# Transfers that add into on-chip memory in place of some VectorE sums of weight blocks, and a new order of some products

## The chip, the cores and the metric

The kernel runs on one core of one Trainium2 chip. The metric is the device time of one execution in microseconds (us). It is compared with the time of the kernel before, which is 1497.2 us (median of three runs, 1497.01 to 1497.43).

## The reference

The reference is one layer of a hybrid decoder: a token mixer with two parallel branches, and a squared-ReLU MLP. 256 tokens and 16 learned meta tokens pass through it, with 2048 channels, all in float32.

```python
def hybrid_mixer(xn, w_in, ...):
    proj = xn @ w_in                                  # 2048 x 13336
    ...                                               # forgetting attention, gated linear attention
    y = jax.nn.sigmoid(gate_fox) * (o_fox @ w_o_fox) + jax.nn.sigmoid(gate_gla) * (o_gla @ w_o_gla)
    return y @ w_out
def squared_relu_mlp(xn, w1, w2):                     # 2048 -> 8192 -> 2048
    return jnp.square(jax.nn.relu(xn @ w1)) @ w2
...
    h = h + hybrid_mixer(rmsnorm(h, norm_mix_g[l]), ...)
    h = h + squared_relu_mlp(rmsnorm(h, norm_mlp_g[l]), w_ff1[l], w_ff2[l])
```

Nearly all of the work is matrix products of 256 tokens with large weight matrices. Every weight is read once from HBM.

## The kernel before

**Precision.** Each float32 operand is split into a high part, which ScalarE (ACT) rounds to TensorE's reduced float32, and a low part, which VectorE (DVE) forms as value minus high part. A product is then three matmuls: high by high, high by low, low by high. For weights this split is `cut` (lines 968 to 974): the cast on ACT is line 972 and the subtraction on DVE line 973. It reads a raw tile of 128 x 1024 floats (512 KB) and writes a tile `w`. There are five `raw` buffers and five `w` buffers.

**Stages.** The input projection, both branches and their heads come first, up to about 480 us. From 480 to 698 us `columns` makes, for three groups `b` of output columns, the branch projections (`lone`, tiles `gla` and `fox`) and the two gates (a pair, below). Then the last columns of the mixer and the output projection run to about 840 us, and from there to 1440 us the MLP runs as fifteen pairs. The last output columns and the final norm end the kernel.

**A pair** (`pair_of`) multiplies the operand with two groups of four blocks of 128 columns, `f1` and `f2 = f1 + 4`. The tokens are two halves of 128. The contraction over 2048 runs in steps of 256. A plain step (`plain`) loads one raw tile, splits it, and makes two products of six matmuls of 512 columns, one for each half of the tokens. For the first 512 (one form) or the first 1024 (two forms) of the contraction, a Strassen-Winograd form makes seven products of six matmuls where plain steps make eight. With r11, r21 the weights of `f1` and r12, r22 those of `f2` in the two halves of these 512, a form multiplies

- own tokens with r11 (`m1`), r21 (`m2`), and r21 less the weight sum of `m6` (`m4`);
- sums of tokens, made ahead by `token_sums`, with r12 - r11 (`m5`), r22 - (r12 - r11) (`m6`), r22 - r12 (`m7`) and r22 (`m3`).

The weight sums are made by `less` (line 977): one DVE operation over a whole 128 x 1024 tile. `held` loads r12 and r22 into tiles that stay (`hb`, `hc`; with a second form also `hd`, and `he`, which is the tile `sums4` in the MLP and shows as `sums` in the profile). The fifteen pairs of the MLP are twelve with one form and three with two (`nq == 2`); the three pairs of `columns` have two forms as well. That makes twelve pairs with one form and six with two.

**What sets the order.** SyncE (SP) issues the weight loads in program order; each waits until its `raw` buffer is free, which is when the DVE has read it. ACT and DVE run in order. While the plain steps of one pair run, the steps of the next pair are put between them by lists of places: the `n`-th number is the plain step after which step `n` of the next pair is emitted. Lines 1149 and 1152 hold the lists of `columns`, line 1367 those of the MLP, by `index % 4` of the running pair; `index % 4 == 2` is where the steps of a pair with two forms are emitted. A planner with its own times may move instructions of an engine against each other where nothing forbids it; `keep_in_program_order` holds the results of `less` in place.

**GpSimd (POOL)** has little to do here. Once for each group of the MLP it reloads saved token sums from HBM (line 1378: four transfers of 256 KB, `s_x<-kept_sums`), each waiting until TensorE has used the old ones.

Of the kernel before, what the change touches and what calls it, by code (L numbers as in the profile page):

```python
# [12 lines left out]
ALU = mybir.AluOpType  # L13
# [3 lines left out]
P = 128  # L17
# [56 lines left out]
def trunk(ctx: ExitStack, tc: tile.TileContext, hT, w_small, w_all, consts, w_alpha2, out):  # L74
    nc = tc.nc
# [236 lines left out]
    x = x_row[:, :, NM : NM + 2 * NT].rearrange("p k (o t) -> p k o t", t=NT)  # L312
# [85 lines left out]
    for s in range(KT // 2):  # L398
# [5 lines left out]
        for kk in range(2):  # L404
            k = 2 * s + kk
# [496 lines left out]
    def token_sums(dst, src, temp):  # L902

        v = temp.rearrange("p (s k m) -> p s k m", s=4, m=P)
        c, d = (v[:, i].rearrange("p k (c r) -> p k c r", r=32) for i in (0, 1))
        s3, s4 = (v[:, i].rearrange("p k (c r) -> p k c r", r=32) for i in (2, 3))
        nc.vector.tensor_tensor(c, src(0, 1), src(1, 1), op=ALU.add)
        nc.vector.tensor_tensor(s3, src(0, 0), src(0, 1), op=ALU.subtract)
        nc.vector.tensor_tensor(d, c, src(0, 0), op=ALU.subtract)
        nc.vector.tensor_tensor(s4, src(1, 0), d, op=ALU.subtract)  # L910
        split_to(dst[:, :, :, 0, :], dst[:, :, :, 1, :], v)

# [60 lines left out]
        made(copied, nc.vector.tensor_tensor(lo, r, hi.bitcast(F32), op=ALU.subtract).ins, 1)  # L973
        return [t.rearrange("p k c m -> p k (c m)") for t in (hi, lo)]

    def less(dst, a, b):
        tc.keep_in_program_order(nc.vector.tensor_tensor(dst, a, b, op=ALU.subtract))

    hold_pool = [None]
    held_at = {}  # L980
# [1 line left out]
    def holder(tag):  # L982
        if tag in held_at:
            return held_at[tag]
        return hold_pool[0].tile([P, HK * P], F32, tag=tag, name=nm(tag))
# [13 lines left out]
    def pair_of(f1, x, sums, evict, even, by_rows=False, low=False):  # L999
# [12 lines left out]
        def product(n, xs, w, start=False):  # L1012
            product_into(bk(n), xs, w, start)

        def own(t, k0):
            return tokens(x, t, k0)

        def split_of(raw):
            return cut(raw, low)
# [9 lines left out]
        nq = len(sums)  # L1029

        def held(q):
            got["b", q], got["c", q] = fetched(f2, 4 * q, ("hb", "hd")[q]), fetched(f2, 4 * q + 2, ("hc", "he")[q])

        def m1(q):
            r11 = fetched(f1, 4 * q)
            w = split_of(r11)
            got["a", q] = r11 if nq > 1 else holder("hd")
            less(got["a", q], got["b", q], r11)
            product("x", own(0, 4 * q), w, q == 0)
            if q == nq - 1:  # L1040
                nc.scalar.copy(bk("y"), bk("x"))

        def m5(q):
            w = split_of(got["a", q])
            if nq > 1:
                less(got["b", q], got["c", q], got["b", q])
                less(got["c", q], got["c", q], got["a", q])
            else:
                less(got["a", q], got["c", q], got["a", q])
            product("v", summed(q, 0), w, q == 0)  # L1050
            if q == nq - 1:
                got["m5"] = hold_pool[0].tile([P, 512], F32, tag="m5", name=nm("m5"))
                nc.scalar.copy(got["m5"], bk("v"))

        def m6(q):
            w = split_of(got["c" if nq > 1 else "a", q])
            if nq == 1:
                less(got["b", q], got["c", q], got["b", q])
            product("x", summed(q, 1), w)
            if q == nq - 1:  # L1060
                nc.vector.tensor_tensor(bk("z"), bk("x"), got["m5"], op=ALU.add)
# [9 lines left out]
        def m2(q):  # L1071
            r21 = fetched(f1, 4 * q + 2)
            w = split_of(r21)
            t2 = got["c" if nq > 1 else "a", q]
            less(t2, r21, t2)
            product("y", own(0, 4 * q + 2), w)

        def m4(q):
            product("x", own(1, 4 * q + 2), split_of(got["c" if nq > 1 else "a", q]))

        if nq == 1:
            firsts = [(m, 0) for m in (held, m1, m5, m6, m7, m3, m2, m4)]
# [22 lines left out]
    def columns():  # L1105
# [40 lines left out]
            work += made_pairs[b][1]  # L1146
            work += [lambda b=b, k=k: lone(b, "fox", k) for k in range(0, KT // 2, 2)]
        at = {}
        for n, i in enumerate((-1, 1, 1, 2, 3, 4, 5, 5, 6, 7, 8, 8, 9, 9, 10, 12)):
            at.setdefault(i, []).append(made_pairs[0][0][n])  # L1150
        for b in (1, 2):
            for n, i in enumerate((-5, -4, -3, -1, 0, 2, 3, 4, 5, 6, 7, 8, 9, 10, 10, 12)):
# [211 lines left out]
    while rest_now:  # L1364
        key, make = next(coming, (None, None))
        steps_next, rest_next = make() if make else ([], [])
        at = {1: (0, 3, 4, 5, 6, 8, 9, 10), 2: (0, 2, 1, 2, 4, 5, 5, 6, 7, 7, 8, 8, 9, 9, 10, 11),
              3: (0, 2, 4, 5, 5, 6, 6, 7)}.get(index % 4, (0, 2, 3, 4, 5, 7, 9, 10))
        if index == 0:
            steps_now[7]()  # L1370
        closing = index == 4 * NG - 3
        for i, run in enumerate(rest_now):
            run()
            if index == 0 and i == 2:
                norm2()
            if index % 4 == 3 and i == 0:
                for q in range(4):
                    nc.gpsimd.dma_start(s_x2[:, q].bitcast(F32), kept_sums[:, q])
            for n, step in enumerate(steps_next):
                if at[n] == i and closing and n > 4:  # L1380
                    late.append(step)
                elif at[n] == i:
                    step()
            if not steps_next and i in (1, 3, 5):
                late.pop(0)()
        issued()
        rest_now, index = rest_next, index + 1
# [169 lines left out]
```

## Time and profile before

| | |
|---|---|
| median of three runs | 1497.2 us |
| the profiled execution, its own time | 1497.08 us |
| its span, first to last instruction | 1495.1 us |
| TensorE (PE) busy | 1484.9 us |
| PE weight loads (PEld) busy | 1322.2 us |
| VectorE (DVE) busy | 1193.2 us |
| ScalarE (ACT) busy | 878.4 us |
| GpSimd (POOL) busy | 119.8 us |
| moved by DMA | 335.00 MB |

Matmuls overlap in the array, so a single one shows some 380 ns while the next starts 220 ns after it. A row of the timeline gives start, duration, engine, line, operation, output and inputs, how many such instructions follow each other, and in brackets the idle time before them with what ended it. "Landing" is the time from the issue of a transfer to its completion.

### The profile page before, as it was taken

The numbers are of one execution on the slowest core, as the hardware profiler recorded it, in microseconds if no ns is written. First come the engines' busy times: TensorE is split into PE (matmuls) and PEld (weight loads), VectorE is DVE, ScalarE is ACT, GpSimd is POOL, SyncE is SP. The second block draws the span as 40 slices with busy tenths as digits, with TensorE's granted clock in tenths as the row PEclk, the third lists the DMA queues.
The fourth block names the chain that finished last, engine by engine and source line by source line (L and its number), as shares of the span: only waits on it lengthen the run. The fifth ranks groups of instructions, "written<-read, shape, count | busy, mean of one in ns | idle before, by whom it ended". The sixth has DMA issues, their size and how long they took to land.

```text
span 1495.1 us, 22541 instructions
## 1 busy us (share of the span) xinstructions
PE 1484.9 (99%) x8374; PEld 1322.2 (88%) x8374; DVE 1193.2 (80%) x1578; ACT 878.4 (59%) x1246; POOL 119.8 (8%) x202
## 2 busy tenths in 40 slices
PE   9999999999999999999999999999999999999997
PEld 8999999999999888888988888888888888888887
DVE  7899858586677877876788889877998889898766
ACT  7765444455555555555566666666665566556645
POOL 6012100111111000000011100000000000000004
PEclk9999999999999999999999999999999999999999
DMA  9545555465547677678678678877777778888783
GB/s 325 176 145 185 182 170 180 159 213 170 169 163 247 212 224 233 205 230 286 223 248 253 204 248 264 267 230 242 250 244 249 230 250 252 266 260 273 249 277 110
DMA packets 242545, 335.00 MB, mean 224 GB/s; under 512 B 13130, under 2 KB 209748, under 8 KB 242180
## 3 DMA queue, kind: packets, MB, share of 16 engines
q1 hardware_dynamic: 219940, 299.22, 61.2%
q10 hardware_dynamic: 21360, 30.09, 6.5%
q0 software_dynamic: 1136, 4.27, 0.9%
q8 instruction: 65, 1.06, 0.3%
q14 instruction: 44, 0.36, 0.1%
HBM read 316.22 MB, written 17.31 MB: 223 GB/s over the span
## 4 chain that ended last, share of the span: by engine, by line
PE 96%; DVE 2%; issue 1%; ACT 1%; POOL 0%; POOLq 0%; DVEq 0%; ACTq 0%
PE bx L993 17%; PE ps L169 14%; PE bv L993 11%; PE by L993 11%; PE bz L993 11%; PE ps L170 7%; PE psa L174 5%; PE psa L178 5%; PE psa L176 4%; PE gla L993 4%; PE fox L993 2%; PE ps L429 1%; PE ps L431 1%; PE ps L1424 1%; DVE w L135 1%
## 5 line engine op out<-in xcount | busy, mean ns | idle before, releaser
L973 DVE TENSOR_TENSOR w<-raw,w 128x1024 fp32r<-128x1024 f32 x300 | 365.4, 1224 | 100.9 <-ACT w L972 96.6
L972 ACT CAST w<-raw 128x1024 fp32r<-128x1024 f32 x300 | 312.3, 1048 | 203.6 <-PE bx L993 68.2
L135 DVE TENSOR_TENSOR w<-raw,w 128x1024 fp32r<-128x1024 f32 x198 | 243.0, 1229 | 81.5 <-ACT w L134 80.1
L134 ACT CAST w<-raw 128x1024 fp32r<-128x1024 f32 x198 | 207.4, 1049 | 92.4 <-PE psa L178 30.3
L169 PE MATMUL ps<-x,w 128*128 128x512 f32 x543 | 184.4, 383 | 0.0
L174 PE MATMUL psa<-x,w 128*128 128x272 f32 x640 | 181.7, 285 | 0.0
L178 PE MATMUL psa<-x,w 128*128 128x272 f32 x640 | 179.6, 282 | 0.0
L176 PE MATMUL psa<-x,w 128*128 128x272 f32 x624 | 175.9, 282 | 0.0
L170 PE MATMUL ps<-x,w 128*128 128x256 f32 x543 | 149.0, 274 | 0.0
L993 PE MATMUL bx<-w,x 128*128 128x512 f32 x528 | 131.1, 381 | 0.0
L174 PEld LDWEIGHTS psa<-x,w 128*128 128x128 f32 x640 | 120.2, 188 | 0.2
L178 PEld LDWEIGHTS psa<-x,w 128*128 128x128 f32 x640 | 120.2, 188 | 0.1
L176 PEld LDWEIGHTS psa<-x,w 128*128 128x128 f32 x624 | 117.4, 188 | 0.0
L169 PEld LDWEIGHTS ps<-x,w 128*128 128x128 f32 x543 | 101.9, 188 | 17.1
L993 PEld LDWEIGHTS bx<-w,x 128*128 128x128 f32 x528 | 98.8, 188 | 17.4
L993 PE MATMUL by<-w,x 128*128 128x512 f32 x444 | 112.5, 381 | 0.0
L170 PEld LDWEIGHTS ps<-x,w 128*128 128x128 f32 x543 | 102.0, 188 | 0.0
L993 PEld LDWEIGHTS by<-w,x 128*128 128x128 f32 x444 | 83.2, 188 | 14.6
L993 PE MATMUL bv<-w,x 128*128 128x512 f32 x360 | 91.9, 381 | 0.0
L993 PE MATMUL bz<-w,x 128*128 128x512 f32 x360 | 91.6, 381 | 0.0
L169 PE MATMUL ps<-y,w 128*128 128x512 f32 x256 | 85.6, 380 | 0.0
L993 PE MATMUL bx<-w,a 128*128 128x512 f32 x336 | 83.7, 380 | 0.0
(405 smaller groups left out, 2741.1 us busy)
## 6 DMA issues: line engine op xcount, KB each, us to landing
raw<-w_all_dram SPq DMA_DIRECT2D x489, 512.0 KB, 4.6
there<-turn ACTq DMA_DIRECT2D x80, 128.0 KB, 3.9
turn<-there ACTq DMA_DIRECT2D x20, 512.0 KB, 4.7
hb<-w_all_dram SPq DMA_DIRECT2D x18, 512.0 KB, 4.4
hc<-w_all_dram SPq DMA_DIRECT2D x18, 512.0 KB, 5.3
raw<-w_all_dram SPq DMA_DIRECT2D x26, 256.0 KB, 5.0
raw<-w_all_dram SPq DMA_DIRECT2D x8, 384.0 KB, 6.8
hd<-w_all_dram SPq DMA_DIRECT2D x6, 512.0 KB, 7.1
```

The source lines that it names most:

```text
L134: copied = nc.scalar.copy(hi[:, k, :], r).ins
L135: return copied, nc.vector.tensor_tensor(lo[:, k, :], r, hi[:, k, :].bitcast(F32), op=ALU.subtract).ins
L169: nc.tensor.matmul(steps(ps), hi, steps(row(x)), start=first, stop=False)
L170: nc.tensor.matmul(steps(ps[:, 0:NT]), lo, steps(x[:, 0, :]), start=False, stop=last)
L174: nc.tensor.matmul(steps(ps[:, X_LO]), hi, steps(x_lo[:, k]), start=first, stop=False, skip_group_check=True)
L176: nc.tensor.matmul(steps(ps[:, 0:NA]), lo, steps(x_hi[:, k]), start=False, stop=last and hi is None, skip_group_check=True)
L178: nc.tensor.matmul(steps(ps[:, 0:NA]), hi, steps(x_hi[:, k]), start=False, stop=last, skip_group_check=True)
L429: nc.tensor.matmul(steps(ps), hi, steps(row(x[:, k])), start=st, stop=False)
L431: nc.tensor.matmul(steps(ps[:, 0:NT]), lo, steps(x[:, k, 0]), start=False, stop=sp)
L972: copied = nc.scalar.copy(hi, r).ins
L973: made(copied, nc.vector.tensor_tensor(lo, r, hi.bitcast(F32), op=ALU.subtract).ins, 1)
L993: nc.tensor.matmul(steps(ps), l, steps(r), start=start and k == 0 and i == 0, stop=False, skip_group_check=True)
```

## The change

The signs of the form change, so that r22 is added in two of its weight sums: `m6` now takes r22 + (r12 - r11), and `m7` takes r12 + r22. The token sums change their signs to match, with the same four operations. This lets r22 be added by a DMA that accumulates into its destination (`gain_block`, issued by GpSimd):

- in each form, r22 is added to the tile that holds r12, once `m1`'s `less` has read it (before: a `less` on DVE);
- in pairs with two forms, r22 is also added to the tile that holds r12 - r11, once `m5`'s split has read it (before: a `less` on DVE). In pairs with one form this sum stays on DVE, now as an addition;
- in pairs with two forms, r22 isn't loaded by `held` any more, and r12 of the second form takes the tile `hc`. The difference r12 - r11 goes to `hd` or `he` instead of r11's own `raw` tile;
- the lists of places of the first pair of `columns`, and of the MLP's pairs with two forms, change.

The number of matmuls, casts and splits is the same.

```diff
-        nc.vector.tensor_tensor(c, src(0, 1), src(1, 1), op=ALU.add)
-        nc.vector.tensor_tensor(s3, src(0, 0), src(0, 1), op=ALU.subtract)
-        nc.vector.tensor_tensor(d, c, src(0, 0), op=ALU.subtract)
+        nc.vector.tensor_tensor(c, src(0, 1), src(1, 1), op=ALU.subtract)
+        nc.vector.tensor_tensor(s3, src(0, 1), src(0, 0), op=ALU.subtract)
+        nc.vector.tensor_tensor(d, src(0, 0), c, op=ALU.subtract)
...
-    def less(dst, a, b):
-        tc.keep_in_program_order(nc.vector.tensor_tensor(dst, a, b, op=ALU.subtract))
+    def less(dst, a, b, op=ALU.subtract):
+        tc.keep_in_program_order(nc.vector.tensor_tensor(dst, a, b, op=op))
+
+    def gain_block(raw, c0, k0):
+        nc.gpsimd.dma_start(raw.rearrange("p (c k m) -> p c k m", k=2, m=P),
+                            w_all[c0 : c0 + 4, :, k0 * P : (k0 + 2) * P].rearrange("c p (k m) -> p c k m", m=P),
+                            accum_op=ALU.add)
...
         def held(q):
-            got["b", q], got["c", q] = fetched(f2, 4 * q, ("hb", "hd")[q]), fetched(f2, 4 * q + 2, ("hc", "he")[q])
+            got["b", q] = fetched(f2, 4 * q, ("hb", "hc")[q])
+            if nq == 1:
+                got["c", q] = fetched(f2, 4 * q + 2, "hc")
...
-            got["a", q] = r11 if nq > 1 else holder("hd")
+            got["a", q] = holder(("hd", "he")[q])
             less(got["a", q], got["b", q], r11)
+            gain_block(got["b", q], f2, 4 * q + 2)
...
         def m5(q):
             w = split_of(got["a", q])
             if nq > 1:
-                less(got["b", q], got["c", q], got["b", q])
-                less(got["c", q], got["c", q], got["a", q])
+                gain_block(got["a", q], f2, 4 * q + 2)
             else:
-                less(got["a", q], got["c", q], got["a", q])
+                less(got["a", q], got["c", q], got["a", q], ALU.add)
...
         def m6(q):
-            w = split_of(got["c" if nq > 1 else "a", q])
-            if nq == 1:
-                less(got["b", q], got["c", q], got["b", q])
+            w = split_of(got["a", q])
...
-            t2 = got["c" if nq > 1 else "a", q]
+            t2 = got["a", q]
...
-            product("x", own(1, 4 * q + 2), split_of(got["c" if nq > 1 else "a", q]))
+            product("x", own(1, 4 * q + 2), split_of(got["a", q]))
...
-        for n, i in enumerate((-1, 1, 1, 2, 3, 4, 5, 5, 6, 7, 8, 8, 9, 9, 10, 12)):
+        for n, i in enumerate((-1, 0, 1, 1, 2, 3, 5, 6, 6, 7, 8, 8, 9, 9, 10, 12)):
...
-        at = {1: (0, 3, 4, 5, 6, 8, 9, 10), 2: (0, 2, 1, 2, 4, 5, 5, 6, 7, 7, 8, 8, 9, 9, 10, 11),
+        at = {1: (0, 3, 4, 5, 6, 8, 9, 10), 2: (0, 1, 1, 2, 3, 4, 5, 7, 7, 8, 8, 8, 9, 9, 10, 11),
```

## The prediction

> **What bounds the kernel now.** I read the page first: the busy times, then the engines of the chain of waits that ended last.
>
> ```profile
> span 1495.1 us, 22541 instructions
> ...
> PE 1484.9 (99%) x8374; PEld 1322.2 (88%) x8374; DVE 1193.2 (80%) x1578; ACT 878.4 (59%) x1246; POOL 119.8 (8%) x202
> ```
>
> ```profile
> PE 96%; DVE 2%; issue 1%; ACT 1%; POOL 0%; POOLq 0%; DVEq 0%; ACTq 0%
> ```
>
> The reader is to see that TensorE (PE) is busy in all but 10.2 us of the span and holds 96% of the chain. A busy PE could still be a slow one, because matmul ends are modelled. So I checked its pace, in the chain of waits in order of time (start, us, what).
>
> ```profile
> 549.60 5.34 PE fox L993 x24
> ...
> 621.75 5.34 PE fox L993 x24
> ```
>
> ```profile
> 926.76 2.64 PE bx L993 x12
> ...
> 1251.47 2.64 PE bx L993 x12
> ```
>
> Twelve matmuls in 2.64 us are 0.220 us each. One group of the MLP is three pairs with one form and one pair with two. A pair with one form has 7 x 6 + 12 x 12 = 186 matmuls, one with two has 14 x 6 + 8 x 12 = 180; together 738, and 738 x 0.220 = 162.36 us. The same place of the schedule stands at 926.76 and, two groups on, at 1251.47: 324.71 us, or 162.36 a group. So PE never falls out of step by even one matmul there. In `columns` one group has 96 + 180 + 48 = 324 matmuls and takes 621.75 - 549.60 = 72.15 us, 0.2227 each: the whole excess over 0.220 is 0.87 us a group.
>
> Next I read the engines by stretch (PE, PEld, DVE, ACT, POOL busy, granted clock, DMA share, GB/s), one group of `columns`, then the stretch in which a pair with two forms is prepared, then the one after it, then the one with the heaviest DMA.
>
> ```profile
> 542.90:615.10 72.20, 72.20 (x326) 60.73 (x325) 55.85 (x52) 38.75 (x40) 0.00 (x0) 1.00 0.71 226
> 923.00:975.00 52.00, 52.00 (x239) 44.35 (x238) 44.56 (x43) 33.37 (x38) 2.22 (x4) 1.00 0.85 263
> 975.00:1007.00 32.00, 32.00 (x147) 27.32 (x146) 25.52 (x23) 19.57 (x22) 0.00 (x0) 1.00 0.67 216
> 1325.00:1368.00 43.00, 43.00 (x197) 36.69 (x196) 37.13 (x38) 25.53 (x29) 0.00 (x0) 1.00 0.95 305
> ```
>
> PE fills every stretch, at the full granted clock. DVE has 14% to 23% of room, DMA 5% to 33%. Last the waits: those of PE, and the longest of ACT's cast.
>
> ```profile
> PE warm L393 <- DVE ones L274: 1.3, 1, 1.3
> ```
>
> ```profile
> ACT w L972 <- PE bx L993: 95.2, 100, 2.7
> ```
>
> The first is the longest wait of PE, at the very start; from 480 to 1465 us its list is empty. ACT instead waits for PE, 100 times by this row alone, for a free `w` buffer. So the splits run ahead of PE by as much as five buffers allow, and a faster DVE only waits longer.
>
> **The change, part by part.** *Removed sums.* The rows of `less` that go (the form, then first and last start):
>
> ```profile
> L977 DVE TENSOR_TENSOR hb<-hc,hb x18: 1209/1219/1758, 483.7 to 1381.8; 128x1024 f32<-128x1024 f32 x18
> ```
>
> ```profile
> L977 DVE TENSOR_TENSOR hc<-hc,raw x6: 1214/1218/1226, 485.9 to 1254.1; 128x1024 f32<-128x1024 f32 x6
> ```
>
> ```profile
> L977 DVE TENSOR_TENSOR hd<-he,hd x3: 1218/1219/1219, 493.7 to 631.8; 128x1024 f32<-128x1024 f32 x3
> L977 DVE TENSOR_TENSOR he<-he,raw x3: 1212/1216/1218, 496.0 to 635.2; 128x1024 f32<-128x1024 f32 x3
> ```
>
> ```profile
> L977 DVE TENSOR_TENSOR hd<-sums,hd x3: 1218/1218/1220, 937.8 to 1262.6; 128x1024 f32<-128x1024 f32 x3
> L977 DVE TENSOR_TENSOR sums<-sums,raw x3: 1217/1218/1219, 940.1 to 1264.8; 128x1024 f32<-128x1024 f32 x3
> ```
>
> That is 18 + 6 + 3 + 3 + 3 + 3 = 36 operations (12 pairs x 1, 6 pairs x 4) of 1.219 us: 43.9 us off DVE's 1193.2. None of it is on the path, since PE waits for no split. Gain: 0.
>
> *Transfers.* The same 36 sums become accumulating transfers of 512 KB on GpSimd's queue. SP loses 12 loads of 512 KB (`hd` 6, `he` 3, `sums` 3).
>
> ```profile
> hd<-w_all_dram SPq DMA_DIRECT2D x6, 512.0 KB, 7.1
> s_x<-kept_sums POOLq DMA_DIRECT2D x12, 256.0 KB, 4.6
> ...
> he<-w_all_dram SPq DMA_DIRECT2D x3, 512.0 KB, 4.8
> ...
> sums<-w_all_dram SPq DMA_DIRECT2D x3, 512.0 KB, 5.7
> ```
>
> So 24 x 0.524 = 12.6 MB more come from HBM. The stretch at 0.95 with 305 GB/s puts a full share at 321 GB/s, so 512 KB cost 1.63 us of all sixteen engines. No row shows an accumulating transfer. Its load on the engines is at least that of a plain one (k = 1); it also has to read its destination, which makes k = 2 natural, and k = 3 is my upper bound (source, destination and write each counted as a whole transfer). In the stretch of two forms, 0.85 x 52 = 44.2 us are taken; the change there is four accumulations less two loads, 1.63 x (4k - 2): 47.5 us at k = 1, 54.0 at k = 2, 60.5 at k = 3. I take k = 2: 2.0 us over, which the lead of the splits covers (4.5 us, below). Cost: 0; without that cover 3 x 2.0 = 6 us.
>
> The page "Collectives: The Full Stack" of the Trainium skill, section "The bandwidth ceiling: the fold count and why AG ≠ RS ≠ AR", speaks against the change: an add inside a DMA engine reads two sources per chunk and halved the rate of its ring. By it the stage would be at 54.0 of 52 us; by plain transfers at 47.5. No run here shows an accumulation yet.
>
> *The new wait.* ACT's cast for `m7` (and, with two forms, for `m6`) now waits for the landing. ACT is in order: behind it stand the next casts, the copies of `bx` and `m5`, and the activations of the MLP; DVE waits for those casts, PE for both. How long may it take from the release of the transfer to its landing, T, before PE is late? A split needs cast and subtraction, 1.05 + 1.22 = 2.27 us, before PE starts. Rows of the timeline at the three kinds of place, first `columns` (second form of the second group; its lists are unchanged):
>
> ```profile
> 558.50 1.22 DVE L973 TENSOR_TENSOR w<-raw,w 128x1024 fp32r<-128x1024 f32 x1
> ```
>
> ```profile
> 565.72 1.05 ACT L972 CAST w<-he 128x1024 fp32r<-128x1024 f32 x1 [0.62 <-PE gla L993]
> ```
>
> ```profile
> 571.26 0.38 PE L993 MATMUL bx<-w,s_x 128*128 128x512 f32 x1
> ```
>
> `m5`'s split has read its source at 559.72; PE wants `m6` at 571.26. T may be 571.26 - 2.27 - 559.72 = 9.3 us, and 6.0 us before ACT itself, ready at 565.72, stands still. There are two such places (groups 1 and 2). Next a pair with one form (twelve places): the transfer is released by `hd<-hb,raw`, the sum ends in `m7`.
>
> ```profile
> 884.84 1.22 DVE L977 TENSOR_TENSOR hd<-hb,raw 128x1024 f32<-128x1024 f32 x1
> ```
>
> ```profile
> 900.20 1.48 PE L993 MATMUL bx<-w,s_a 128*128 128x512 f32 x6
> ```
>
> T may be 900.20 - 2.27 - 886.06 = 11.9 us. Last the second form of a pair with two in the MLP (three places):
>
> ```profile
> 936.70 1.22 DVE L973 TENSOR_TENSOR w<-raw,w 128x1024 fp32r<-128x1024 f32 x1 [1.19 <-ACT w L972]
> ```
>
> ```profile
> 942.44 1.48 PE L993 MATMUL bv<-w,s_x 128*128 128x512 f32 x6
> ```
>
> ```profile
> 945.52 0.38 PE L993 MATMUL bx<-w,s_x 128*128 128x512 f32 x1
> ```
>
> The split of `m5` ends at 937.92, 4.5 us before PE wants it (942.44): that is the lead. With the old places T would be 945.52 - 2.27 - 937.92 = 5.3 us. The new list moves `m5` from place 5 to 4 and `m6` from 6 to 7, two plain steps of 2.64 us further apart: 10.6 us. Without the new places the same T = 7 would stop PE for 1.7 us in each.
>
> T itself is bounded below by 4.6 us (the row of `s_x`: GpSimd's queue, half the bytes) and above by two of the slowest plain loads one after the other, 2 x 7.1 = 14.2 us. I take the row nearest in kind, the same queue: 4.6 + 0.8 (the other 256 KB) + 1.6 (the destination's read) = 7.0 us. That is under 9.3, 10.6 and 11.9: no matmul is late; in `columns` ACT stands 1.0 us and catches up. Cost: 0.
>
> *GpSimd's queue.* An accumulation must not stand behind a reload of the saved sums. The last reload of a group, and the `less` that releases the next accumulation:
>
> ```profile
> 973.25 0.54 POOL L1378 DMA_DIRECT2D s_x<-kept_sums  x1 [15.30 <-PE bz L993]
> ```
>
> ```profile
> 974.60 1.22 DVE L977 TENSOR_TENSOR hd<-hb,raw 128x1024 f32<-128x1024 f32 x1
> ```
>
> The queue is free at 973.8, the transfer is released at 975.8. An issue takes 0.54 us here; 36 are 19 us on an engine that is 8% busy. Should one take three times that, with its smaller pieces, T grows by 1.1 us and stays below 9.3. Cost: 0.
>
> *Places, and r11's buffer.* The order of some products changes, not their number: 0 on PE, where what it needs is there. The new places of the first group of `columns` leave three plain steps between `m5` and `m6`, more than in the other groups. r11 no longer holds a `raw` buffer until `m5`'s sums are done, so loads start earlier. Gain: 0, for the same reason as above.
>
> *Sum.* 1497.08 us (the profiled execution: span 1495.1 and 2.0 around it) + 0. The median of the runs is 0.1 us above that execution; I forecast 1497.2 us.
>
> **The rivals.** *The landing is too slow* (slower). If T is above 9.3, PE waits in `columns`, from 10.6 in the MLP's two forms, from 11.9 in all twelve other pairs. At T = 12 that is 2 x 2.7 + 3 x 1.4 + 12 x 0.1 = 10.8 us: 1508. At 14.2 it is 9.8 + 10.8 + 27.6 = 48 us: 1545. It decides from T = 10.8 on (2 x 1.5 us = 3). For it: `hd`, a plain load issued among others, takes 7.1, and the engines are at 0.71 to 0.95. Against it: twice 7.1 needs the destination's read to wait for the whole source.
>
> *DMA becomes the bound* (slower). At k = 3 the stretch of two forms needs 60.5 us in 52, 8.5 over; less the lead of 4.5 that is 4 us in each of three: 12 us, 1509. It decides from 44.2 + 1.63 x (4k - 2) = 52 + 4.5 + 1, so k = 2.7. For it: the stretch at 0.95, which also gets an accumulation. Against it: 0.67 in the stretch behind lets it catch up.
>
> *A faster pace in `columns`* (faster). If the new order took the 0.2227 down to the MLP's 0.220, 3 x 0.87 = 2.6 us would go: 1494.6. Against it: that pace is there in all three groups, in plain steps and forms, and lists change in one group. It is less than 3 us even then.
>
> *The change doesn't do what it says*: the planner could keep the old order around the transfers. With the old places T may be 5.3 in three places; at 7.0 that costs 3 x 1.7 = 5 us: 1502.
>
> **How the numbers follow.** A measurement of this kernel tells 0.2%, 3.0 us, from no change. Forecast (PE stays full): 0.70, of it 0.68 within 0.2%. Landing too slow: 0.14. DMA the bound: 0.08. Old order kept: 0.04. Faster pace: 0.04, half of which I let reach beyond 3 us together with the small stalls at the start of `columns`. So faster 0.04 (0.02 from there and 0.02 from the forecast's edge), same 0.70 (0.68 and 0.02), slower 0.26. The forecast's own range is 1495 to 1499. The range for 8 in 10 goes down to 1494.5 (the pace) and up to 1506 (T near 11.5, and the old order kept); it leaves out the upper halves of the two slower rivals, some 0.13, and little below.
>
> **What would show it.** Right: PE's list of waits stays empty between 480 and 1465 us, and the same places of two groups are 162.4 us apart; DVE busy is near 1149 us; the 36 transfers on POOL's queue land in about 7 us; ACT shows some waits for them, and more for PE. Wrong: waits of PE for DVE at `m6` in `columns` first (landing), or casts that wait for `raw` transfers in the stretches of two forms with a DMA share near 1 (k). A time above 1500 with T below 9 would break the working itself: then something I have as covered, order or queue, is not.

## The result, and the profile after

The changed kernel takes 1511.72 us (median of 4 runs, 1507.63 to 1516.84); beside it the kernel before takes 1497.11 us (1496.91 to 1497.43). The ratio is 1.0097, with a 95% interval of 1.0082 to 1.0112: the change makes the kernel 1% slower. The forecast of no change was wrong, and the measured median lies above its range too. The profiled execution of the changed kernel is its fastest one, 1507.63 us; what follows explains that one, and the others as far as the runs allow. Two slow executions in the experiments below, one of ten with the forced order (1524.83 us) and one of four with the old places (1543.49 us), are left out of the ratios and ranges given there.

The page of the changed kernel, the same lines as were read before:

```profile
span 1505.4 us, 22609 instructions
...
PE 1488.0 (99%) x8374; PEld 1320.8 (88%) x8374; DVE 1152.6 (77%) x1542; ACT 874.7 (58%) x1246; POOL 165.9 (11%) x238
...
PE 85%; DMA 4%; issue 4%; DVE 4%; ACT 2%; POOL 1%; SPq 0%; POOLq 0%; DVEq 0%; ACTq 0%
```

DVE lost 40.6 us, where 43.9 were forecast, and the span grew by 10.3 us. The chain that ended last is no longer TensorE's alone: DMA, DVE and the issue of instructions hold 12% of it. TensorE's list of waits between 480 and 1465 us, empty before, now reads:

```profile
PE by L998 <- DVE w L973: 3.2, 3, 1.1
PE bx L998 <- DVE w L973: 1.5, 2, 0.8
PE by L998 <- ACT w L972: 0.9, 3, 0.3
PE bx L998 <- ACT w L972: 0.3, 1, 0.3
```

The counts say where: one such place in each of three groups. To get the sizes I took the start of the k-th instruction of TensorE in each profile and subtracted its start in the kernel before (both kernels have 8374). Columns: the time of that instruction before, in us; the lower row: how much later it starts in the changed kernel, in us.

```
before    44    483    594    650    703    937    992   1102   1157   1267   1322   1432
later   0.69   0.68   0.58   0.38  -0.17  -0.17   2.43   2.43   6.39   6.39  10.03  10.03
```

The 0.69 us arise in the first 44 us, where nothing was changed (such offsets of up to 0.8 us appear in several of the profiles below). Then there are three steps: 2.60, 3.96 and 3.64 us, together 10.20. They are the second forms of the three MLP pairs with two forms. Between them the twelve pairs with one form cost nothing. `columns` even gains 0.85 us, and that gain is explained further below.

The first of the three places, on four engines. GpSimd issues the accumulations (start, us, line, what, and in brackets the idle time before and what ended it):

```profile
923.11 1.29 POOL L980 DMA_DIRECT2D hb<-w_all_dram  x1 [34.53 <-ACT turn L1319]
926.18 1.29 POOL L980 DMA_DIRECT2D hd<-w_all_dram  x1 [1.77 <-DVE w L973]
931.68 1.27 POOL L980 DMA_DIRECT2D hc<-w_all_dram  x1 [4.21 <-DVE sums L977]
934.50 1.27 POOL L980 DMA_DIRECT2D sums<-w_all_dram  x1 [1.55 <-DVE w L973]
```

The last of them is released when DVE has read `sums` for `m5`, at 932.98 + 1.23 = 934.21:

```profile
932.98 1.23 DVE L973 TENSOR_TENSOR w<-sums,w 128x1024 fp32r<-128x1024 f32 x1 [0.46 <-ACT w L972]
```

ACT needs what has landed, for `m6`:

```profile
948.13 1.05 ACT L972 CAST w<-sums 128x1024 fp32r<-128x1024 f32 x1 [5.93 <-DMA sums<-w_all_dram]
```

T, from release to landing, is 948.13 - 934.21 = 13.9 us. The products of `m6` start as soon as this split is there, at 950.49, some 0.2 us late. TensorE's longer waits are for the splits that stood behind it on ACT and DVE:

```profile
952.17 0.49 PE L998 MATMUL by<-w,a 128*128 128x512 f32 x1 [0.28 <-ACT w L972]
...
953.96 1.42 PE L998 MATMUL by<-w,a 128*128 128x512 f32 x5 [1.08 <-DVE w L973]
```

The last of these rows shows 1.08 us of idle time, but it starts 1.47 us after the product before it instead of 0.22, so it costs 1.25 us: behind a gap the overlap with the product before is gone. That is why the waits in the list above add up to 5.9 us and the three steps to 10.20.

In the other two groups the rows of the release and of the cast are:

```profile
1097.94 1.23 DVE L973 TENSOR_TENSOR w<-sums,w 128x1024 fp32r<-128x1024 f32 x1 [0.46 <-ACT w L972]
...
1264.26 1.23 DVE L973 TENSOR_TENSOR w<-sums,w 128x1024 fp32r<-128x1024 f32 x1 [0.47 <-ACT w L972]
```

```profile
1114.47 1.05 ACT L972 CAST w<-sums 128x1024 fp32r<-128x1024 f32 x1 [6.05 <-DMA sums<-w_all_dram]
...
1280.46 1.05 ACT L972 CAST w<-sums 128x1024 fp32r<-128x1024 f32 x1 [6.22 <-DMA sums<-w_all_dram]
```

There T is 1114.47 - 1099.17 = 15.3 us and 1280.46 - 1265.49 = 15.0 us. Less the steps of 2.60, 3.96 and 3.64 us this leaves 11.3 us in each of the three: a single allowed time, and beyond it every microsecond of T is a microsecond of the kernel.

Why T is so long is seen in the landings of all 36 (KB each, median us from issue to landing), beside the plain loads of the same size:

```profile
raw<-w_all_dram SPq DMA_DIRECT2D x489, 512.0 KB, 4.8
...
hb<-w_all_dram POOLq DMA_DIRECT2D x18, 512.0 KB, 8.9
...
hd<-w_all_dram POOLq DMA_DIRECT2D x6, 512.0 KB, 10.3
hc<-w_all_dram POOLq DMA_DIRECT2D x6, 512.0 KB, 10.5
...
he<-w_all_dram POOLq DMA_DIRECT2D x3, 512.0 KB, 10.5
...
sums<-w_all_dram POOLq DMA_DIRECT2D x3, 512.0 KB, 14.6
```

It is `sums`, the fourth in its place, that is slowest. The records of single packets show the reason. An accumulation is 512 packets of 1024 bytes, and a packet takes 101 ns (median) where a plain packet of 1024 bytes takes 46. In the first place (us):

```
                 issued   first packet   last packet ends
hb (m1, form 1)  923.11      926.40          931.27
hd (m5, form 1)  926.18      931.18          936.91
hc (m1, form 2)  931.68      936.83          941.46
sums (m5, f. 2)  934.50      941.38          947.65
```

Each one starts when the one before it ends: GpSimd's queue carries one accumulation at a time, some 5.3 us each in this place. `sums`, which is needed first, is issued 2.8 us after `hc`, which ACT casts only three splits later (at 952.02), and its first packet comes 6.9 us after its issue, where 2.1 us were enough on a free queue (`hb` of the second group of `columns`, issued at 542.27, first packet at 544.36).

### The profile page after: what moved, and what is told of

The parts are those of the page before. It is cut to its first block, busy times and chain, and to the rows that moved or that the text cites. A ratio compares the mean times of both kernels' runs of the same rounds, so it can differ in the third digit from the quotient of the medians.

```text
span 1505.4 us, 22609 instructions
## 1 busy us (share of the span) xinstructions
PE 1488.0 (99%) x8374; PEld 1320.8 (88%) x8374; DVE 1152.6 (77%) x1542; ACT 874.7 (58%) x1246; POOL 165.9 (11%) x238
## 4 chain that ended last, share of the span: by engine, by line
PE 85%; DMA 4%; issue 4%; DVE 4%; ACT 2%; POOL 1%; SPq 0%; POOLq 0%; DVEq 0%; ACTq 0%
PE bx L998 14%; PE ps L169 14%; PE by L998 9%; PE bz L998 9%; PE bv L998 8%; PE ps L170 7%; PE psa L174 5%; PE psa L178 5%; PE psa L176 4%; PE gla L998 3%; DMA sums<-w_all_dram 3%; PE fox L998 2%; PE ps L429 1%; ACT w L972 1%; DVE w L973 1%
## 5 line engine op out<-in xcount | busy, mean ns | idle before, releaser
L973 DVE TENSOR_TENSOR w<-raw,w 128x1024 fp32r<-128x1024 f32 x288 | 351.1, 1225 | 96.5 <-ACT w L972 92.0
L972 ACT CAST w<-raw 128x1024 fp32r<-128x1024 f32 x288 | 299.7, 1047 | 174.2 <-PE bv L998 56.3
L135 DVE TENSOR_TENSOR w<-raw,w 128x1024 fp32r<-128x1024 f32 x198 | 242.9, 1228 | 82.6 <-ACT w L134 81.1
L134 ACT CAST w<-raw 128x1024 fp32r<-128x1024 f32 x198 | 207.4, 1049 | 93.6 <-PE psa L178 30.2
L973 DVE TENSOR_TENSOR w<-hd,w 128x1024 fp32r<-128x1024 f32 x54 | 66.0, 1222 | 30.2 <-ACT w L972 29.5
L972 ACT CAST w<-hd 128x1024 fp32r<-128x1024 f32 x54 | 56.5, 1046 | 52.0 <-DVE hd L977 16.2
```

Source lines behind the costliest of these rows:

```text
L134: copied = nc.scalar.copy(hi[:, k, :], r).ins
L135: return copied, nc.vector.tensor_tensor(lo[:, k, :], r, hi[:, k, :].bitcast(F32), op=ALU.subtract).ins
L972: copied = nc.scalar.copy(hi, r).ins
```

## The experiments

Three theories stood at the start. *Queue*: four accumulations of one pair follow each other on one queue, so the fourth lands too late. *Load*: an accumulation costs the DMA engines twice a plain load, and the stages with two forms have no room for it. *Places*: the new places of the products, not the transfers, cost the time.

**Fewer accumulations.** The accumulation only in the twelve pairs with one form; the pairs with two forms take their sums on DVE as before, with the new signs, and all products have their old places:

```diff
-            got["b", q] = fetched(f2, 4 * q, ("hb", "hc")[q])
-            if nq == 1:
-                got["c", q] = fetched(f2, 4 * q + 2, "hc")
+            got["b", q], got["c", q] = fetched(f2, 4 * q, ("hb", "hd")[q]), fetched(f2, 4 * q + 2, ("hc", "he")[q])
...
-            gain_block(got["b", q], f2, 4 * q + 2)
+            if nq == 1:
+                gain_block(got["b", q], f2, 4 * q + 2)
...
-                gain_block(got["a", q], f2, 4 * q + 2)
+                less(got["b", q], got["c", q], got["b", q], ALU.add)
+                less(got["c", q], got["c", q], got["a", q], ALU.add)
...
```

> Transfers that accumulate in the twelve pairs with one form only; the six pairs with two forms make their sums on DVE as before (with the new signs) and have the old places. The changed kernel loses 10.5 us of PE starts, all but 0.7 us of it in the three MLP pairs with two forms. Theory Q (the four accumulations of a pair with two forms stand one behind another in GpSimd's queue): 12 accumulations, never two close together, each landing in 8 to 9 us against 11.9 allowed: no stall, 1497.1 us. Theory L (the DMA engines as a whole are full around the pairs with two forms): 1497.1 too, since those pairs are as before. If accumulating transfers cost PE something by themselves (a slower pace, a wait on them in pairs with one form): about a third of the loss, 1500 or more.

Measured: 1497.46 us (1496.98 to 1499.26) against 1497.66; ratio 0.9999 (0.9990 to 1.0009). TensorE has no wait between 480 and 1465 us.

Next, 24 of the 36: `m1`'s accumulation everywhere, `m5`'s not, at the new places. Its sum is on DVE, from an r22 that `held` loads and keeps as in the kernel before. A pair with two forms then has two accumulations instead of four:

```diff
...
-                gain_block(got["a", q], f2, 4 * q + 2)
+                less(got["c", q], got["c", q], got["a", q], ALU.add)
...
```

> Only the accumulation into r12 stays (one per form, 24 in all); the sum for m6 is made on DVE from an r22 that is loaded and held, as before. Places are the new ones. Theory Q: in a pair with two forms two accumulations stand in the queue instead of four, and both are needed only for m7, some 15 us after their release: no stall, 1497 to 1498 us. Theory L: the load on the engines around a pair with two forms falls from 20 plain loads and 4 accumulations at 2.2 each (28.8 units) to 22 and 2 (26.4; before 22): about a third of the stall goes, 1504 us or more. Theory P (the new places of the products are what hurts): as the changed kernel, 1507 to 1517 us.

Measured: 1497.65 us (1497.00 to 1498.08); ratio 0.9999 (0.9990 to 1.0008). Its profile, the stretch around the first of the three places, then the landings:

```profile
925.00:980.00 55.00, 55.00 (x251) 46.92 (x251) 44.52 (x42) 33.78 (x37) 5.78 (x7) 1.00 0.93 280
```

```profile
hb<-w_all_dram POOLq DMA_DIRECT2D x18, 512.0 KB, 8.4
hd<-w_all_dram POOLq DMA_DIRECT2D x6, 512.0 KB, 8.5
```

TensorE is busy for all 55 us, and the second of a pair lands as fast as the first: they are issued 8.2 us apart (924.66 and 932.86), so the queue is free again. The places are the new ones and cost nothing; *places* falls.

**The transfers without the add.** The 36 transfers stay where they are but overwrite their destination, so the sums of the weights are left out:

```diff
-                            w_all[c0 : c0 + 4, :, k0 * P : (k0 + 2) * P].rearrange("c p (k m) -> p c k m", m=P),
-                            accum_op=ALU.add)
+                            w_all[c0 : c0 + 4, :, k0 * P : (k0 + 2) * P].rearrange("c p (k m) -> p c k m", m=P))
```

> The 36 transfers on GpSimd's queue are plain copies: r22 overwrites the tile instead of being added, so the sums are left out. Packets of 1024 bytes should take 46 ns instead of 101, a transfer 1.6 us of all engines instead of 3.3. Theory Q: four transfers in a row take half as long, the fourth lands in about 8 us: 1497 to 1499 us. Theory L: the load falls from 28.8 units to 24: most of the stall goes, 1497 to 1500 us. If the queue of GpSimd is slow whatever the transfer does (issue and descriptors): landings stay near 9 and 14 us and the time near 1507 to 1517 us. Theory P: 1507 to 1517 us.

Measured: 1497.70 us (1497.40 to 1499.34); ratio 1.0003 (0.9993 to 1.0012). The landings:

```profile
hb<-w_all_dram POOLq DMA_DIRECT2D x18, 512.0 KB, 6.5
...
sums<-w_all_dram POOLq DMA_DIRECT2D x3, 512.0 KB, 7.3
```

With the same number, waits and places of the transfers, but packets of 4096 bytes at 159 ns, the fourth in a row lands after 7.3 us and no step is left. These transfers go one after another too, but in the first place in 3.2 to 3.6 us each, where the accumulations took 4.6 to 6.3. It is the accumulation itself that makes the queue slow, not its wait. The smaller packets alone don't explain it: 512 plain ones of 46 ns are 1.5 us of sixteen engines, 128 of 159 ns are 1.3, and 512 of 101 ns are 3.2.

**The order in the queue.** The second form's `m1` accumulation (`hc`) behind that form's `m5` accumulation (`sums`), which is needed first:

```diff
-            gain_block(got["b", q], f2, 4 * q + 2)
+            if q == 0:
+                gain_block(got["b", q], f2, 4 * q + 2)
...
                 gain_block(got["a", q], f2, 4 * q + 2)
+                if q == 1:
+                    gain_block(got["b", q], f2, 4 * q + 2)
```

> All 36 accumulations stay; only the order on GpSimd's queue changes: the second form's accumulation into r12 (needed for m7) is issued after that form's accumulation into r12 - r11 (needed for m6, which comes first). Load on the engines and places are those of the changed kernel. Theory Q: the late transfer starts one transfer earlier, so it lands about 5 us earlier (9 instead of 14.6 us after its release); ACT's wait for it falls from 6 us to 1 and PE's loss of 3.5 us in each of three places goes: 1497 to 1500 us. Theory L: the same bytes in the same stretch, as the changed kernel, 1507 to 1517 us. Theory P: the same, 1507 to 1517 us.

Measured: 1514.22 us (1510.91 to 1517.20); 1.0110 (1.0093 to 1.0126). The planner put the transfers back into the old order, though, as GpSimd's issues show:

```profile
932.20 1.27 POOL L980 DMA_DIRECT2D hc<-w_all_dram  x1 [4.21 <-DVE sums L977]
935.03 1.27 POOL L980 DMA_DIRECT2D sums<-w_all_dram  x1 [1.55 <-DVE w L973]
```

It says nothing on the order; it is the changed kernel's queue once more, and its steps are there again. With the order forced on the planner:

```diff
...
-                gain_block(got["a", q], f2, 4 * q + 2)
+                first = gain_block(got["a", q], f2, 4 * q + 2)
+                if q == 1:
+                    with tc.issue_after(first.ins):
+                        gain_block(got["b", q], f2, 4 * q + 2)
```

> As the swap before, with the order now forced: the second form's accumulation into r12 is issued after the one into r12 - r11 (the planner had put them back, so that run was a second run of the changed kernel). Load on the engines and places are those of the changed kernel. Theory Q (one behind another in GpSimd's queue): the transfer that is late starts one transfer earlier and lands 5 us earlier, some 9 us after its release; ACT's wait for it falls from 6 us to about 1 and the 3.5 us in each of three places go: 1497 to 1500 us. Theory L (the load of the engines in that stretch, whatever the order): 1507 to 1517 us.

Measured: ratio 1.0041 (1.0030 to 1.0052), single runs from 1497.76 to 1506.46 us. The profiled one took 1504.86. Its first place:

```profile
935.47 1.27 POOL L980 DMA_DIRECT2D sums<-w_all_dram  x1 [7.35 <-DVE w L973]
936.22 1.83 POOL L980 DMA_DIRECT2D hc<-w_all_dram  x1
```

```profile
946.40 1.05 ACT L972 CAST w<-sums 128x1024 fp32r<-128x1024 f32 x1 [4.02 <-DMA sums<-w_all_dram]
```

```profile
925.00:980.00 55.00, 55.00 (x251) 46.66 (x250) 41.41 (x39) 33.77 (x39) 7.48 (x9) 1.00 1.02 285
```

`sums` now lands 11.2 us after its release (933.96 + 1.22 = 935.18), just under the 11.3 allowed, and TensorE is busy throughout. The DMA engines are as full as they can be (1.02 in this view) with all four accumulations in the stretch, and nothing is late. So *queue* holds, and *load* alone does not stop TensorE here. The fastest execution of this run, 1497.76 us, is even within those of the kernel before beside it (1496.69 to 1499.16). But the profiled one is still 7.5 us longer than the kernel before. The shifts of the k-th instruction, as above, here and in the run with the planner's order:

```
before             483    703    937    992   1102   1157   1267   1322   1377   1432   1472
order forced      0.48   0.48   0.48   0.70   0.70   1.09   1.09   3.01   5.10   7.18   7.48
planner's order   0.36   0.35   0.35   4.51   6.18   9.80   9.80  14.05  14.71  15.38  15.45
```

The three places cost only 0.2 to 0.4 us with the forced order. After the third, however, the shift grows steadily, by 2.08 us in 250 instructions. The chain in order of time shows it (start, us, what):

```profile
1276.32 1.32 PE bx L998 x6
...
1280.52 0.03 issue
1280.54 3.00 PE bx L998 x12
1283.54 1.37 PE bz L998 x6
```

Six products of 512 columns take 1.32 us before the small gap and 1.37 behind it, up to the end of the pairs. Start to start, the products go from 220.0 to 228.3 ns, 8.3 ns more for each, and that is nearly all of the 6.4 us by which the shift grows behind the third place (7.48 less 1.09). The granted clock is 1.00 on both sides. No step of the prediction and none of the three theories has such a thing.

**The old places.** The changed kernel with the lists of places of the kernel before:

```diff
-        for n, i in enumerate((-1, 0, 1, 1, 2, 3, 5, 6, 6, 7, 8, 8, 9, 9, 10, 12)):
+        for n, i in enumerate((-1, 1, 1, 2, 3, 4, 5, 5, 6, 7, 8, 8, 9, 9, 10, 12)):
...
-        at = {1: (0, 3, 4, 5, 6, 8, 9, 10), 2: (0, 1, 1, 2, 3, 4, 5, 7, 7, 8, 8, 8, 9, 9, 10, 11),
+        at = {1: (0, 3, 4, 5, 6, 8, 9, 10), 2: (0, 2, 1, 2, 4, 5, 5, 6, 7, 7, 8, 8, 9, 9, 10, 11),
```

> The changed kernel with the lists of places of before. Theory P (the new places hurt): 1497 to 1500 us. Theory Q: the products that wait for the late transfer come two plain steps, 5.3 us, earlier in each of the three MLP pairs, and the loss grows by up to that: 3.5 + 5.3 in each, 1518 to 1526 us; in the first group of columns up to 2 us more.

Measured: ratio 1.0181 (1.0144 to 1.0218), single runs from 1519.62 to 1531.43 us; the profiled run took 1519.62 us. By the shifts of the k-th instruction each of the three places now costs 5.7 to 6.3 us, and the first group of `columns` 4.1. One of the places:

```profile
953.56 0.49 PE L998 MATMUL bx<-w,s_x 128*128 128x512 f32 x1 [2.70 <-ACT w L972]
...
955.23 2.33 PE L998 MATMUL bx<-w,s_x 128*128 128x512 f32 x5
```

Between the profiled executions, the places that give `m6` more time are worth 12.0 us (1519.62 less 1507.63). After 2.7 us of waiting, TensorE's next products take 0.427 us each, twice their time: its granted clock is 0.50 from 955 to 958 us, and the same is seen behind the waits of the other places. So a long wait costs more than itself. In the changed kernel, with no wait above 1.1 us there, the clock stays at 1.00.

**The gain side alone.** The kernel before with its 36 sums left out, nothing in their place:

```diff
-                less(got["b", q], got["c", q], got["b", q])
-                less(got["c", q], got["c", q], got["a", q])
+                pass
...
-            if nq == 1:
-                less(got["b", q], got["c", q], got["b", q])
```

> The kernel before with the 36 DVE sums left out and nothing in their place: the products take unsummed weights, all matmuls, casts, splits and loads stay. It measures the gain side alone. The forecast's step (none of the 43.9 us is on the path) says 1497.1 us, within 0.1%. If DVE does set the pace anywhere: 1496 us or less.

Measured: 1497.52 us (1497.20 to 1498.00); 1.0001 (0.9991 to 1.0010), with DVE at 1154.5 us. Taking 38.7 us off DVE is worth nothing that can be measured.

**The pace of the products.** From here on the question is the steady pace that changed at a small gap. In the kernel before, the products of 512 columns follow each other every 222.7 ns in `columns` (a repeating pattern of 217 to 228) and every 220.0 in the MLP, with hardly an exception. First: one short extra product ahead of the first product of each bank, with a different number of columns each time:

```diff
+    shorts = []
+    SHORT = (128, 256, 64, 384, 192, 448, 320)
...
+                if start and k + i == 0:
+                    n = SHORT[len(shorts) % len(SHORT)]
+                    shorts.append(n)
+                    if n:
+                        nc.tensor.matmul(steps(ps[:, 0:n]), l, steps(r[:, 0:n]), start=True, stop=False,
+                                         skip_group_check=True)
```

> The kernel before, with one thing added: ahead of the first product of every bank that a pair or a lone part of the columns opens (48 places: 18 in the columns, 30 in the MLP) one extra product of the same weights into the same bank, with fewer columns (128, 256, 64, 384, 192, 448 and 320 in turn; the next product opens the bank again, so nothing of it stays in the result). No transfer and no sum is changed. Theory F (each stage has its own pace, and an irregularity costs only itself): 48 products of 256 columns on the mean, by 220 ns for 512, are 5.3 us, so 1501.5 to 1504; the products of 512 columns stay at 222.7 ns in the columns and 220.0 in the MLP. Theory R (an irregularity in the stream of products sets the pace that holds until the next one): the pace changes from one opened bank to the next; the columns run at 220.0 in some stretches, the MLP at 222 to 228 in others; as all 3200 products of 512 columns at 220.0 would give 1500 and a third of them at 228.3 would give 1509, the time is anywhere from 1499 to 1515, and the profile shows at least two paces in the MLP.

Measured: 1507.87 us (1507.43 to 1507.94); 1.0071 (1.0054 to 1.0088), above what fixed paces allow. The chain at one of the places, with a short product of 128 columns on the added line, L999:

```profile
1156.78 1.32 PE bv L1002 x6
1158.10 0.06 PE bv L999
...
1159.55 1.34 PE bz L1002 x6
```

The extra product takes 0.06 us and leaves the rest at 223.3 ns, in the MLP, until the next short one. Over the whole run, behind 64 and 256 columns the pace was always 220.0 (6 and 7 places that can be read), behind 384 always 223.3 (7 places), and behind 128, 192, 320 and 448 sometimes the one, sometimes the other.

Then a single one in the whole MLP, 384 columns:

```diff
+    opened = []
...
+                if start and k + i == 0:
+                    opened.append(1)
+                    if len(opened) == 22:
+                        nc.tensor.matmul(steps(ps[:, 0:384]), l, steps(r[:, 0:384]), start=True, stop=False,
+                                         skip_group_check=True)
```

> The kernel before with one product added in the whole MLP: ahead of the first product of bv in the first pair (at about 857 us) a product of the same weights over 384 columns into the same bank, which the next product opens again. From there on the kernel before has some 2660 products of 512 columns at exactly 220.0 ns and no gap. Theory R: in the earlier run every product of 384 columns was followed by 223.3 ns; if that holds until the end of the pairs, 2660 x 3.3 ns = 8.8 us and 0.2 us for the product itself come on top: 1506.2 (1505.5 to 1507). Theory F: the product's own 0.2 us, 1497.4.

Measured: 1506.94 us (1506.34 to 1507.02); 1.0061 (1.0048 to 1.0075). The chain at the place (the added product is L997), which has 1.32 us for six products on one side and 1.34 on the other:

```profile
852.10 1.32 PE bx L1000 x6
...
854.30 0.17 PE bv L997
854.46 1.34 PE bv L1000 x6
```

The shift grows evenly from here, 0.83 us in 250 instructions, to 9.0 us at the end of the pairs: a product of 0.17 us cost 9.3 with what follows it (1506.94 less 1497.64, the kernel before beside it). The edit adds nothing but this one product.

Third, `columns`. One product split into two at about 506 us, into 64 and 448 columns and, in a second kernel, into 256 and 256:

```diff
...
-                    nc.tensor.matmul(steps(ps), l, steps(r), start=start and k == 0 and i == 0, stop=False,
-                                     skip_group_check=True)
+                    for c in ((slice(0, 64), slice(64, 512)) if split and k + i == 0 else (slice(0, 512),)):
+                        nc.tensor.matmul(steps(ps[:, c]), l, steps(r[:, c]), start=start and k == 0 and i == 0,
+                                         stop=False, skip_group_check=True)
...
+                             (which, b, k0, t) == ("gla", 0, 12, 0))
```

> The kernel before with one product of the columns (lone gla of b=0, k0=12, the first product of the first token half, after the last guest in the columns' stream, so at about 506 us) written as two over 64 and 448 columns; the result is the same. Before, 830 products of 512 columns between 505 and 690 us follow each other every 222.7 ns. Theory R (an irregularity sets the pace until the next one): after the earlier run's products of 64 columns the pace was 220.0 ns in every case, so 830 x 2.7 ns = 2.2 us are saved against 0.1 us for the split: 1495.0 (1494.8 to 1495.4). Theory F (the columns have their own pace, from their operands): 1497.3, and 222.7 ns stays.

> The same as the run with 64 and 448 columns, but cut into 256 and 256. Theory R: in the earlier run 220.0 ns followed every product of 256 columns too, so 1495.0 again; where this cut keeps the pace at 222.7 the time is 1497.3 and what decides is the offset that the cut leaves, not that there is one. Theory F: 1497.3.

Measured: 1499.67 us each, 1.0020 (1.0011 to 1.0029) and 1.0015 (1.0006 to 1.0024), which neither theory had. Both cuts move `columns` from 222.7 to 223.3 ns and not to 220.0, and in both another 1.6 us go between 703 and 787 us, before the MLP takes up its 220.0 again: an irregularity changes the pace, but its length does not say to which.

Last, two short products of 64 columns in `columns`, ahead of banks that open at 543 and 556 us (the edit as above, with `len(opened) in (5, 9)` and 64 columns):

> The kernel before with two products of 64 columns added in the columns, each ahead of the first product of a bank that the next product opens again: the lone fox part of b=0 (about 544 us) and the lone gla part of b=1 (about 558 us). Nothing else is changed. In the run with a short product at every opened bank, each of the products of 64 columns was followed by 220.0 ns; the cuts into 64 and 448 columns were not. Theory R1 (64 columns ahead of an opened bank always give 220.0): from 545 to 690 us 650 products x 2.7 ns = 1.75 us are saved, two products cost 0.1 us each: 1495.9 against 1497.4 before. Theory R2 (what comes depends on the offsets before it too, so a length alone does not fix it): any of the paces seen (220.0, 222.7, 223.3), 1495.9 to 1498.5, and the run's profile shows which.

Measured: 1495.70 us (1495.27 to 1496.41) against 1497.54; ratio 0.9989 (0.9980 to 0.9998). The chain, to be held beside the prediction's 5.34 us for the same 24 products:

```profile
543.03 0.03 PE fox L997
...
549.74 5.28 PE fox L1000 x24
```

24 products in 5.28 us are 220.0 ns each. The k-th instruction, 0.1 us late at 538, is 1.5 us early from 703 on. This version, the kernel before with two useless products more, is faster than both kernels of the case.

## Why the prediction was wrong, point by point

*What bounds the kernel, and the removed sums*: right. TensorE's stream was the bound, DVE's 43.9 us were covered, and the run with the sums left out shows the gain of 0.

*Transfers*: k = 2 was about right. A packet costs 101 ns instead of 46, which is 2.2, and an accumulation takes 3.2 to 3.7 us of all sixteen engines where 3.26 were forecast. The rule of the page "Collectives: The Full Stack" of the Trainium skill, section "The bandwidth ceiling: the fold count and why AG ≠ RS ≠ AR", that was quoted there, of a rate halved by the add, agrees with this. The DMA share of the stretch is at its ceiling in the run with the forced order, and the lead of the splits covered it.

*The new wait*: this is the step that failed, in its choice of T = 7.0 us. It is too short even for one accumulation alone. In the run with accumulations in the pairs with one form only, none stands behind another, and they land 9.5 us after their issue:

```profile
hb<-w_all_dram POOLq DMA_DIRECT2D x12, 512.0 KB, 9.5
```

Against the 11.9 us allowed there, that was hidden, so this error alone cost nothing. What cost time is the place in the queue. The step that looked at *GpSimd's queue* asked whether an accumulation stands behind a reload, and not whether it stands behind another accumulation, although the sum for the DMA engines before it counted four in one stretch. In `columns` (second group) T was 10.8 us (the split of `m5` ends at 561.16, the cast starts at 571.93):

```profile
559.98 1.18 DVE L973 TENSOR_TENSOR w<-he,w 128x1024 fp32r<-128x1024 f32 x1
```

```profile
571.93 1.05 ACT L972 CAST w<-he 128x1024 fp32r<-128x1024 f32 x1 [7.15 <-DMA he<-w_all_dram]
```

In the run with the forced order, where the accumulation into `hc` comes behind it, T is still 9.7 us there (560.97 to 570.67). Both are over the 9.3 allowed by the old order, but in the changed kernel the planner had moved `m6` to 574.17, and only 0.1 to 0.4 us were lost. In the MLP's two forms T was 13.9 to 15.3 instead of 7.0, against 10.6 allowed by the forecast and 11.3 found; the upper bound of 14.2, two slow plain loads, was too low as well. The twelve pairs with one form, with one accumulation each, were hidden as forecast.

*GpSimd's issue* was 1.28 us instead of 0.54, 2.4 times, and within the three times allowed for:

```profile
L980 POOL DMA_DIRECT2D hb<-w_all_dram x18: 1273/1290/1363, 480.8 to 1384.2; - x18
```

*The rivals.* "The landing is too slow" came true in the mechanism, at three of its 17 places. It priced one T for all places; with T by place it would have said 3.3 + 4.7 + 4.4 = 12.4 us (T less 10.6 for each of the three), against 10.2 found. "DMA becomes the bound" did not happen. (Its equation for where it decides comes to k = 2.5, not 2.7; the measured 2.2 is below both.) "The change doesn't do what it says" was right in that its condition, the old places, is dear (1.0181), but the change kept the new ones. "A faster pace in `columns`" happened by accident: a gap of 0.09 us at 575.8 took the pace from 222.7 to 220.0, and 0.85 us were gained.

*The rest.* The profiled execution is accounted for: 0.69 at the start, 10.20 in three places, -0.85 in `columns`. The other executions of the changed kernel are 4 to 9 us longer than it. The run with the planner's order, whose accumulations stand in the same order, took 1513.25 us in its profile and shows what can add to it: its three steps come to 12.0 us instead of 10.2, behind the first of its waits the shift grows by 1.67 us between 992 and 1102 us with no gap, behind the third by 1.33 between 1322 and 1432. That the unprofiled executions of the changed kernel are longer for this reason is argued, not shown. What sets the pace stays open; no run here separates it. An offset between weight load and product, which is one guess, is not seen in the records: at every one of the paces, nearly every weight load starts 2 to 4 ns after the start of a product.

## What to carry to other kernels

Where several transfers of one queue fall into one stage, cost the landing of the last in line, not of one alone; the order on the queue should be the order of need, and two transfers fewer in a stage can decide it. Moving work off an engine that nobody waits for earns nothing, and here it bought a wait. In a stream that fills TensorE completely, test the steady distance of the products as well as the gaps: a short wait can cost many times its length in the pace that follows, and the reverse can be had for two small products.

## What the runs showed of the hardware

An accumulating transfer of 512 KB is split into packets of 1024 bytes of 101 ns (median). The same transfer without the add goes in packets of 4096 bytes of 159 ns, so the add costs 2.5 times as much packet time per byte (4 x 101 / 159). The page "DMA: Bandwidth & Descriptors" of the Trainium skill, section "Two DMAs through the same engine are not ordered", says that descriptors of one queue of a DMA engine start in order but are pipelined; these agree on the order, and between two accumulations the packet records of the changed kernel show an overlap of 0.1 us or less, but for the first two (0.26 us).

Products of 512 columns have steady distances of 220.0, 222.7, 223.3 and 228.3 ns at a granted clock of 1.00, each kept over hundreds of products and changed by an irregularity as small as 64 columns. The page "TensorE: Matmul & The Clock Gate", section "Wait — 56ns, not 53.3ns?", gives 215.7 ns for back-to-back matmuls of 512 columns on a warm array, a single value; no steady distance here, where each product has a weight load of its own, is that short. Its 426.7 ns for a cold array agrees with the 427 ns at a granted clock of 0.50 behind the waits of the run with the old places.
